# Second block of a two-block fp32 layer stack: the rescaled residual, the query parts and the sums of squares on VectorE, and five output tiles begun ahead of the attention norm

## The chip, the cores and the metric

The program runs on one core of a Trainium2 chip. The metric is device time in microseconds of the whole program. The time before is the median of three runs, and the profile is of a further execution. The engines are TensorE (PE: matmuls; PEld: its weight loads), VectorE (DVE), ScalarE (ACT), GpSimd (POOL) and SyncE (SP), which issues the DMAs. TensorE runs at one of two clocks, 2.4 or 1.2 GHz; the profile shows the granted one as a share of the full.

## The reference, cut to what matters

The input passes through two layers of a first block, which ends in a norm, then through one layer of a second block, on 512 tokens of width 1024, and at the end a mixture of experts. The second block, where the change is, computes:

```
h = rms_norm(x, ln1_w)                        # x: the first block's result, normed
xr, xg, q, k, v = split(h @ w_in)             # 512 columns each
y_rnn = gelu(xg) * scan(a, u)                 # u, a: gates of a convolved xr; h_t = a_t*h_(t-1) + u_t
y_att = softmax(q k^T / 8 + bias, causal by chunks of 64) v      # 8 heads of 64
x = x + concat(rms_norm(y_rnn, gn_rnn), rms_norm(y_att, gn_att)) @ w_out
x = x + cross_attention(rms_norm(x, ln2_w), rms_norm(mem))       # mem: 256 rows
out = norm(x + experts(rms_norm(x, ln3_w)))
```

## The kernel before, in words

Features lie on the 128 partitions and tokens along the row, so a tile is 128 x 512. A product of two fp32 matrices is made of parts: each operand is split into a rounded high part (ScalarE copies it) and a remainder (subtracted on another engine), and `mm3` adds three matmuls: high by high (line 183), and the two mixed ones (lines 184 and 185). The parts of weights come from `weights` (lines 165 to 180): SP loads a 128x512 piece, ScalarE makes the high part `wh` (line 176), POOL subtracts for the low part `wl` (line 177); the pool has four buffers of each. The parts of data come from `split` (lines 196 and 197) and `scaled_split` (203 and 204), on ScalarE and VectorE. `add_sq` squares a tile on ScalarE (209) and adds it to a sum on POOL (211), or on VectorE if it is told to. A norm is `tok_cols` (713: a matmul with ones adds over the partitions, 4 columns), `rsqrt_cols` (719 on VectorE, 721 on POOL), `bcast` (727: four transposes on TensorE, 729: a copy on VectorE); its result multiplies tiles afterwards.

The second block goes in this order. Four convolutions (line 890 evicts a tile, 893 and 895 are the taps). Then two chains taken in turn: `rnn_gelu` and the query and key tiles of the first four heads (`qk`, two heads a call) beside `rnn_gates` and `rnn_scan`. In `qk` line 872 evicts the query tile; its high part is copied on ScalarE (875) and its remainder made on POOL (876). Line 877 evicts the key tile; lines 879 to 882 make its parts, `kl` on VectorE (881) and its copy on ScalarE (882). `rnn_scan` multiplies (950), scans (951), multiplies by the gelu (952) and adds the square to a sum, which `rnn_norm` uses later. Then the residual is rescaled, eight tiles by a column on ScalarE (1051) and by the broadcast norm on POOL (1052). Then the eight heads, four pieces each: `scores` (978 and 979 on TensorE, 983 adds the bias and takes the maximum on VectorE, 984 is the exponential, 986 the division on VectorE), and `transpose_p` and `outputs` of the piece before. Between them `fill` runs steps of other work by a table: the remaining `qk`, the memory's keys and values (`mem_prep`, `mem_k`, `mem_v`, which takes two accumulators for each half of the columns), and `rnn_norm`. After the last head comes the output projection: eight tiles, each over eight pieces of its input `Y`, four from the recurrence and four from the attention. The first two tiles' recurrent halves go first, then the attention's sum of squares and norm, the scaling of the four attention pieces (1081) and their splits, then the rest; line 1074 adds a tile to the residual.

PSUM has four pools: `pm` of three accumulators for projections, `ps` of two for scores, `px` of two for transposes, `po` of one for head outputs. A scheduler puts each engine's instructions into a fixed order when the program is built, which keeps to dependences but not to the order of the code; at run time each engine goes through its row, and an instruction that waits holds up all behind it on its engine.

Of the kernel before, what the change touches and what calls it, by code (L numbers as in the profile page):

```python
# [15 lines left out]
OP = mybir.AluOpType  # L16
# [111 lines left out]
def body(ctx, tc, a, out, stop=None, dbg=None):  # L128
# [564 lines left out]
    with ExitStack() as c2:  # L693
# [170 lines left out]
        def qk(pr):  # L864
            qs = [slab(F32R, S) for _ in range(2)]
            qf = slab(n=S)
            kf = slab(n=S)
            kh = [slab(F32R, S) for _ in range(2)]
            kl = [slab(F32R, S) for _ in range(2)]
            lo, hi = slice(0, 64), slice(64, 128)  # L870

            yield from proj_g(win(1024 + 128 * pr), X, lambda p: V.scalar_tensor_tensor(qf, p, 0.125, R12, op0=OP.mult,
                                                                                       op1=OP.mult))
            for i, (own, oth) in enumerate(((lo, hi), (hi, lo))):
                ACT(qs[i][own], qf[own], AF.Copy)
                G.tensor_tensor(qs[i][oth], qf[own], qs[i][own].bitcast(F32), op=OP.subtract)
            yield from proj_g(win(1536 + 128 * pr), X, lambda p: V.tensor_tensor(kf, p, R12, op=OP.mult))
            for i, (own, oth) in enumerate(((lo, hi), (hi, lo))):
                ACT(kh[i][own], kf[own], AF.Copy)
                ACT(kh[i][oth], kf[own], AF.Copy)  # L880
                V.tensor_tensor(kl[i][own], kf[own], kh[i][own].bitcast(F32), op=OP.subtract)
                ACT(kl[i][oth], kl[i][own].bitcast(F32), AF.Copy)
            for i in range(2):
                QK[2 * pr + i] = (qs[i], kh[i], kl[i])
# [60 lines left out]
        def rnn_scan():  # L945
            ACT(m24, m24, AF.Sqrt, scale=0.25)
            yield
            for m in range(4):
# [2 lines left out]
                V.tensor_tensor_scan(m2, av, it, 0.0, op0=OP.mult, op1=OP.add)  # L951
                V.scalar_tensor_tensor(it, m2, 0.5, rn["g", m], op0=OP.mult, op1=OP.mult)
                yr.append(it)
                rn["acc"] = add_sq(rn.get("acc"), it, S)
                yield

        def rnn_norm():
# [76 lines left out]

        def mem_v():
            for g in range(2):
                ps = [pm.tile([128, 512], F32, name="pm") for _ in range(2)]
                yield from tokens(lambda k: wmv((g, k)), Xm, 2, ps)
                MV.append([scaled_split(ps[j], rm[:, j:j + 1], n=512) for j in range(2)])

# [5 lines left out]
        Rm = bcast(rm, 2)  # L1046
        run(both(main, side, (2, 1)))
        fillers.extend([qk(2), both(qk(3), mem_prep(), (1, 1)), mem_k(), both(mem_v(), rnn_norm(), (2, 1))])
        for k in range(KT):

            ACT(x2(k), x2(k), AF.Identity, scale=C("final_norm_w")[:, k:k + 1])
            G.tensor_tensor(x2(k), x2(k), R1, op=OP.mult)
        prev = None
        for h in range(8):
            if h + 2 < 8:
                load_bias(h + 2)
            while h not in QK:
                fill()
            for i in range(4):
                e = scores(h, i)  # L1060
                fill(int(STEPS_2[h][i]))
                if prev is not None:
                    transpose_p(*prev)
                    if prev[1] == 3:
                        outputs(prev[0])
                prev = (h, i, e)
        wo = Ahead([(m, wcol(a["w_out_2"][0], 128 * m)) for m in range(8)])
        fill(1000)
        wo(0)
        transpose_p(*prev)  # L1070
        outputs(7)


        outs = [proj_g(wo(m), Y, lambda p, m=m: V.tensor_tensor(x2(m), x2(m), p, op=OP.add)) for m in range(2)]
        for g in outs:
            for _ in range(2):
                next(g)
        ya = [yat[k] for k in range(4)]
        Ra = bcast(rsqrt_cols(tok_cols(sumsq(ya)), 512))
        for m in range(4):  # L1080
            V.scalar_tensor_tensor(ya[m], ya[m], C("gn_att_w_2")[:, m:m + 1], Ra, op0=OP.mult, op1=OP.mult)
            Y[4 + m] = split(ya[m], n=S)
        nrm = Norm(C("ln2_w_2"), S)
        for m in range(8):
            run(outs[m] if m < 2 else proj_g(wo(m), Y, lambda p: V.tensor_tensor(x2(m), x2(m), p, op=OP.add)))
            nrm(m)
        if stop == "b2a":
            nc.sync.dma_start(dbg.rearrange("(k p) t -> p k t", p=128), hT)
# [794 lines left out]
```

## Time and profile before

| | before |
|---|---|
| median of 3 runs | 1425.4 us (1424.39 to 1425.71) |
| profiled execution, its own time | 1425.72 us |
| its span, first to last instruction | 1423.9 us |
| mean granted clock of TensorE | 0.984 |
| TensorE busy | 1353.4 us |
| VectorE busy | 683.4 us, 48% |
| ScalarE busy | 555.1 us, 39% |
| POOL busy | 440.1 us, 31% |

The stretch of the change runs from about 540 us (the end of the first block's norm) to about 815 us. Rows of the timeline give start, duration and count of a run of equal instructions, the engine, line, operation and tiles, and in brackets how long the engine had been idle before and what released it. A matmul's duration overlaps the next one's, so its price is the distance from start to start.

### The profile page before, as it was taken

Reading aid. Unit: us, or ns where it says so; the run is one execution under the profiler, and the core shown is the slowest. Engines: PE = TensorE matmul, PEld = TensorE weight load, DVE = VectorE, ACT = ScalarE, POOL = GpSimd, SP = SyncE. Lnnn points to the kernel's source line nnn. Section 1 sums busy time; section 2 is a strip of 40 time slices with the busy share of each in tenths; the row PEclk is TensorE's granted clock in tenths of the full one; section 3 lists DMA queues with packets and bytes.
Section 4 is the critical chain, followed back from the end, with each engine's and each line's share of the span. In section 5 each row is a group of like instructions: output and inputs, shape, how many; then the busy total and the mean of one; then the engine's idle time right before and its main releaser. Section 6 shows DMA issues by size and latency. Waiting matters only on the chain.

```text
span 1423.9 us, 21255 instructions
## 1 busy us (share of the span) xinstructions
PE 1353.4 (95%) x8236; PEld 1018.1 (71%) x8236; DVE 683.4 (48%) x1305; ACT 555.1 (39%) x1048; POOL 440.1 (31%) x363
## 2 busy tenths in 40 slices
PE   6999999999999999989999999979999999999996
PEld 5998999999899997767876788863454354354343
DVE  5656775455677636777766244252213123132224
ACT  5355554334555562667755344421111110111113
POOL 3432223743222488464477432512000000000002
PEclk9999999999999999999999999989999999999998
DMA  6321112332211242313345122959999999999994
GB/s 202 96 75 40 49 52 84 97 97 66 56 42 58 69 125 81 90 52 120 103 127 175 38 63 91 347 200 382 423 403 423 422 422 423 422 420 422 422 418 154
DMA packets 159288, 279.32 MB, mean 196 GB/s; under 512 B 15568, under 2 KB 127440, under 8 KB 135120
## 3 DMA queue, kind: packets, MB, share of 16 engines
q1 hardware_dynamic: 159184, 277.92, 53.0%
q8 instruction: 66, 1.08, 0.3%
q14 instruction: 38, 0.31, 0.1%
HBM read 275.79 MB, written 2.10 MB: 195 GB/s over the span
## 4 chain that ended last, share of the span: by engine, by line
PE 59%; DVE 7%; DMA 3%; ACT 2%; issue 1%; POOL 1%; DVEq 0%; SPq 0%; POOLq 0%; ACTq 0%
PE pga L1530 7%; PE pgb L1530 7%; PE pm L184 5%; PE pm L185 5%; PE pm L183 5%; PE pgs L1621 4%; PE pgz L1580 3%; PE pgy L1580 3%; PE pgs L1352 3%; PE p L183 2%; PE p L184 2%; PE p L185 2%; DMA ring<-in_expert_gate_w_dram 1%; DMA ring<-in_expert_up_w_dram 1%; DVE slab L197 1%
## 5 line engine op out<-in xcount | busy, mean ns | idle before, releaser
L177 POOL TENSOR_TENSOR wl<-wraw,wh 128x512 fp32r<-128x512 f32 (+1 forms) x248 | 328.1, 1332 | 457.1 <-ACT wh L176 425.2
L176 ACT ACTIVATE wh<-wraw 128x512 fp32r<-128x512 f32 (+1 forms) x248 | 150.6, 616 | 212.6 <-PE pm L184 49.8
L183 PE MATMUL pp<-slab,wh 128*128 128x264 f32 (+1 forms) x536 | 154.8, 290 | 7.6 <-ACT wh L176 6.8
L184 PE MATMUL pp<-slab,wh 128*128 128x264 f32 (+1 forms) x536 | 155.7, 291 | 2.9 <-DVE slab L204 2.7
L185 PE MATMUL pp<-slab,wl 128*128 128x264 f32 (+1 forms) x536 | 154.8, 289 | 1.0 <-POOL wl L177 1.0
L1788 POOL TENSOR_TENSOR ring<-xtok,sel 128x512 f32<-128x512 f32 x4 | 5.0, 1282 | 406.2 <-DVE xtok L1623 406.2
L185 PE MATMUL pm<-slab,wl 128*128 128x512 f32 (+1 forms) x320 | 121.5, 381 | 5.6 <-POOL wl L177 5.5
L184 PE MATMUL pm<-slab,wh 128*128 128x512 f32 (+1 forms) x320 | 120.9, 378 | 2.2 <-DVE slab L197 2.2
L183 PE MATMUL pm<-slab,wh 128*128 128x512 f32 (+1 forms) x320 | 121.1, 380 | 0.0
L183 PE MATMUL p<-slab,wh 128*128 128x264 f32 (+1 forms) x400 | 115.7, 289 | 3.3 <-DVE rs L247 1.6
L1530 PE MATMUL pga<-ring,xT 128*64 128x512 f32 x504 | 116.1, 596 | 0.0
L1530 PE MATMUL pgb<-ring,xT 128*64 128x512 f32 x512 | 113.7, 592 | 0.3 <-DMA ring<-in_expert_up_w_dram 0.3
L185 PE MATMUL p<-slab,wl 128*128 128x264 f32 (+1 forms) x400 | 113.1, 283 | 0.0
L184 PE MATMUL p<-slab,wh 128*128 128x264 f32 (+1 forms) x400 | 112.8, 282 | 0.0
L183 PEld LDWEIGHTS pp<-slab,wh 128*128 128x128 f32 x536 | 103.6, 194 | 8.0 <-ACT wh L176 6.8
L184 PEld LDWEIGHTS pp<-slab,wh 128*128 128x128 f32 x536 | 103.4, 193 | 4.7 <-DVE slab L204 4.2
L185 PEld LDWEIGHTS pp<-slab,wl 128*128 128x128 f32 x536 | 103.8, 194 | 1.5 <-POOL wl L177 1.5
L1530 PEld LDWEIGHTS pgb<-ring,xT 128*64 128x64 f32 x512 | 37.0, 137 | 73.6 <-issue 71.4
L1590 DVE SCALAR_TENSOR_TENSOR yl<-pgy,wcol,yh 128x512 fp32r<-128x512 f32 x16 | 12.0, 751 | 158.2 <-ACT yh L1589 158.2
L1530 PEld LDWEIGHTS pga<-ring,xT 128*64 128x64 f32 x504 | 35.4, 137 | 66.1 <-issue 65.6
L183 PEld LDWEIGHTS p<-slab,wh 128*128 128x128 f32 x400 | 75.5, 189 | 5.1 <-issue 1.7
L184 PEld LDWEIGHTS p<-slab,wh 128*128 128x128 f32 x400 | 75.4, 189 | 0.0
(412 smaller groups left out, 3007.6 us busy)
## 6 DMA issues: line engine op xcount, KB each, us to landing
ring<-in_expert_gate_w_dram SPq DMA_DIRECT2D x63, 1024.0 KB, 17.7
ring<-in_expert_up_w_dram SPq DMA_DIRECT2D x62, 1024.0 KB, 16.2
ring<-in_expert_down_w_dram SPq DMA_DIRECT2D x56, 1024.0 KB, 17.0
wraw<-in_w_in_dram SPq DMA_DIRECT2D x108, 256.0 KB, 2.9
wraw<-in_w_out_dram SPq DMA_DIRECT2D x48, 256.0 KB, 2.9
wraw<-in_xk_w_dram SPq DMA_DIRECT2D x16, 256.0 KB, 2.9
wraw<-in_xv_w_dram SPq DMA_DIRECT2D x16, 256.0 KB, 2.6
wraw<-in_xq_w_dram SPq DMA_DIRECT2D x16, 256.0 KB, 2.9
```

Source lines behind the costliest of these rows:

```text
L176: ACT(h, raw, AF.Copy)
L177: G.tensor_tensor(lo, raw, h.bitcast(F32), op=OP.subtract)
L183: mm(ps, lh, rh, start=first, stop=False)
L184: mm(ps, lh, rl, start=False, stop=False)
L185: mm(ps, ll, rh, start=False, stop=last)
L197: V.tensor_tensor(lo, x, h.bitcast(F32), op=OP.subtract)
L1352: mm(p, h3[:, i, 128 * k:128 * k + 128], sl_[i], start=i == 0 and z == 0, stop=i == 3 and z == 1)
L1530: mm(p[64 * z:64 * z + 64], xt[:, k, CAP * (q + z):CAP * (q + z) + 64], W(src, 2 * pr + z, k), start=k == 0, stop=k == KT - 1)
L1580: mm(ps[c // 512][64 * z:64 * z + 64, c % 512:c % 512 + n], hT_[:, k, 64 * z:64 * z + 64], W("d", 2 * pr + z, k, c, n), start=k == 0, stop ...
L1590: V.scalar_tensor_tensor(yl, p, w[:rows, 0:1], yh.bitcast(F32), op0=OP.mult, op1=OP.subtract)
L1621: mm(p, t[:, 128 * i:128 * i + 128], y, start=q == 0, stop=q == len(ys) - 1)
L1788: G.tensor_tensor(y[i][:, :512], xtok[:, i, :512], fnw[:, :512], op=OP.mult)
```

## The change

It has five parts. (1) The rescale of a residual tile, a ScalarE and a POOL operation, becomes one VectorE operation (line 1054), written in the loop over the heads, one a head. (2) The query remainders, line 876, move from POOL to VectorE. (3) The recurrence's sums of squares move to VectorE; the attention's are added head pair by head pair inside the loop, on VectorE, where before all four stood behind it. (4) The second half of the memory values takes its accumulators from `ps` instead of `pm`. (5) The output projection's weights come in halves, and the recurrent halves of five tiles (three in `pm`, two in `ps`) stand ahead of the attention norm, then the second halves.

```diff
@@ qk @@
                 ACT(qs[i][own], qf[own], AF.Copy)
-                G.tensor_tensor(qs[i][oth], qf[own], qs[i][own].bitcast(F32), op=OP.subtract)
+                V.tensor_tensor(qs[i][oth], qf[own], qs[i][own].bitcast(F32), op=OP.subtract)
@@ rnn_scan @@
-                rn["acc"] = add_sq(rn.get("acc"), it, S)
+                rn["acc"] = add_sq(rn.get("acc"), it, S, eng=V)
@@ mem_v @@
-                ps = [pm.tile([128, 512], F32, name="pm") for _ in range(2)]
+                ps = [(ps_ if g else pm).tile([128, 512], F32, name="ps" if g else "pm") for _ in range(2)]
@@ the rescale, the heads @@
-        for k in range(KT):
-
-            ACT(x2(k), x2(k), AF.Identity, scale=C("final_norm_w")[:, k:k + 1])
-            G.tensor_tensor(x2(k), x2(k), R1, op=OP.mult)
-        prev = None
+        prev = acc = None
         for h in range(8):
...
+            V.scalar_tensor_tensor(x2(h), x2(h), C("final_norm_w")[:, h:h + 1], R1, op0=OP.mult, op1=OP.mult)
...
                         outputs(prev[0])
+                        if prev[0] % 2:
+                            acc = add_sq(acc, yat[prev[0] // 2], S, eng=V)
@@ the output projection @@
-        wo = Ahead([(m, wcol(a["w_out_2"][0], 128 * m)) for m in range(8)])
+        def whalf(m, hf):
+            return lambda: weights(4, [(0, a["w_out_2"][0][512 * hf:512 * hf + 512, 128 * m:128 * m + 128])])
+        NF = 5
+        wo = Ahead([((m, hf), whalf(m, hf)) for ms in (range(NF),) + tuple((m,) for m in range(NF, 8))
+                    for hf in range(2) for m in ms])
...
-        outs = [proj_g(wo(m), Y, lambda p, m=m: V.tensor_tensor(x2(m), x2(m), p, op=OP.add)) for m in range(2)]
-        for g in outs:
-            for _ in range(2):
-                next(g)
+        def out_half(m, hf, p):
+            w = wo((m, hf))
+            for k in range(4):
+                mm3(p, w[k][0], w[k][1], Y[4 * hf + k][0], Y[4 * hf + k][1], hf == 0 and k == 0, hf == 1 and k == 3)
+        po = []
+        for m in range(NF):
+            po.append((pm if m < 3 else ps_).tile([128, 512], F32, name="pm" if m < 3 else "ps"))
+            out_half(m, 0, po[m])
         ya = [yat[k] for k in range(4)]
-        Ra = bcast(rsqrt_cols(tok_cols(sumsq(ya)), 512))
+        Ra = bcast(rsqrt_cols(tok_cols(add_sq(acc, ya[3], S, eng=V)), 512))
...
         for m in range(8):
-            run(outs[m] if m < 2 else proj_g(wo(m), Y, lambda p: V.tensor_tensor(x2(m), x2(m), p, op=OP.add)))
+            if m >= NF:
+                po.append(pm.tile([128, 512], F32, name="pm"))
+                out_half(m, 0, po[m])
+            out_half(m, 1, po[m])
+            V.tensor_tensor(x2(m), x2(m), po[m], op=OP.add)
```

Three places show how the rows of the engines change. The first is POOL at the start of the convolutions, before against after; `hT` is the residual.

```order
 L889 MEMSET slab 128x4
-L1052 TENSOR_TENSOR hT<-hT,slab 128x512 x2
-L177 TENSOR_TENSOR wl<-wraw,wh 128x512
-L1052 TENSOR_TENSOR hT<-hT,slab 128x512 x6
+L177 TENSOR_TENSOR wl<-wraw,wh 128x512 x2
 L889 MEMSET slab 128x4
-L177 TENSOR_TENSOR wl<-wraw,wh 128x512 x3
+L177 TENSOR_TENSOR wl<-wraw,wh 128x512 x2
 L889 MEMSET slab 128x4
```

The eight rescales leave POOL's row, and the weight subtractions follow one another. On VectorE the scheduler sets all eight of line 1054 right behind line 729's copies, ahead of the first eviction of line 890.

The second place is VectorE ahead of the first scores. Before:

```order
L950 TENSOR_TENSOR slab<-slab,m_6821 128x512 x2
L877 TENSOR_TENSOR slab<-pm,slab 128x512
L951 SCALAR_TENSOR_TENSOR m_6821<-slab 128x512 x2
L952 SCALAR_TENSOR_TENSOR slab<-m_6821,slab 128x512 x2
L881 TENSOR_TENSOR slab<-slab 64x512 x2
L872 SCALAR_TENSOR_TENSOR slab<-pm,slab 128x512
L877 TENSOR_TENSOR slab<-pm,slab 128x512
L881 TENSOR_TENSOR slab<-slab 64x512 x2
L983 ISA slab,st_7357<-ps,slab 128x128
```

And after:

```order
L950 TENSOR_TENSOR slab<-slab,m_6821 128x512 x2
L876 TENSOR_TENSOR slab<-slab 64x512 x2
L211 TENSOR_TENSOR slab<-slab 128x512
L877 TENSOR_TENSOR slab<-pm,slab 128x512
L951 SCALAR_TENSOR_TENSOR m_6821<-slab 128x512 x2
L952 SCALAR_TENSOR_TENSOR slab<-m_6821,slab 128x512 x2
L211 TENSOR_TENSOR slab<-slab 128x512
L881 TENSOR_TENSOR slab<-slab 64x512 x2
L872 SCALAR_TENSOR_TENSOR slab<-pm,slab 128x512
L211 TENSOR_TENSOR slab<-slab 128x512
L877 TENSOR_TENSOR slab<-pm,slab 128x512
L876 TENSOR_TENSOR slab<-slab 64x512 x2
```

Four query remainders and three sums are new in the row, partly ahead of the second pair of scans and of line 881.

The third place is TensorE at the attention norm. Before:

```order
L184 MATMUL pm<-slab,wh 128x512
L185 MATMUL pm<-slab,wl 128x512
L713 MATMUL px<-tab,slab 128x1 x4
L183 MATMUL pm<-slab,wh 128x512
L184 MATMUL pm<-slab,wh 128x512
L727 MATMUL px<-tab,rstd_8840 128x128 x4
L185 MATMUL pm<-slab,wl 128x512
```

Behind these stand nine more matmuls of the same tile, and then the first of the attention half. After:

```order
L184 MATMUL ps<-slab,wh 128x512
L185 MATMUL ps<-slab,wl 128x512
L713 MATMUL px<-tab,slab 128x1 x4
L727 MATMUL px<-tab,rstd_8871 128x128 x4
L183 MATMUL pm<-slab,wh 128x512 x3
L183 MATMUL ps<-slab,wh 128x512
L184 MATMUL pm<-slab,wh 128x512
L185 MATMUL pm<-slab,wl 128x512
```

The matmuls that stood between and behind lines 713 and 727 now stand ahead of them, 60 in place of 24, and four tiles instead of three begin on the first attention piece.

## Rows read from the trace of the kernel before

**Rows 1.** The page: busy us, share of the span, instructions.

```profile
PE 1353.4 (95%) x8236; PEld 1018.1 (71%) x8236; DVE 683.4 (48%) x1305; ACT 555.1 (39%) x1048; POOL 440.1 (31%) x363
```

**Rows 2.** Slices: length, busy PE, PEld, DVE, ACT, POOL (count), clock, DMA share, GB/s.

```profile
620.00:640.00 20.00, 13.96 (x54) 10.45 (x53) 16.37 (x17) 13.77 (x24) 17.43 (x11) 0.89 0.14 39
640.00:660.00 20.00, 19.71 (x87) 15.64 (x87) 11.61 (x34) 15.06 (x35) 9.72 (x10) 0.86 0.44 134
660.00:680.00 20.00, 18.85 (x105) 14.95 (x103) 17.48 (x55) 15.43 (x43) 6.67 (x7) 1.00 0.34 105
```

**Rows 3.** TensorE's waits, 540 to 815: us in total, times, longest.

```profile
PE pm L185 <- POOL wl L177: 5.5, 2, 3.2
PE px L994 <- DVE slab L986: 3.1, 5, 0.9
PE pm L183 <- DVE slab L204: 2.2, 1, 2.2
```

**Rows 4.** Timeline of TensorE at the convolutions: start, us, instruction, idle before.

```profile
559.89 0.39 PE L184 MATMUL pm<-slab,wh 128*128 128x512 f32 x1
...
562.57 0.50 PE L185 MATMUL pm<-slab,wl 128*128 128x512 f32 x1 [2.29 <-POOL wl L177]
562.91 0.39 PE L183 MATMUL pm<-slab,wh 128*128 128x512 f32 x1
563.14 0.40 PE L184 MATMUL pm<-slab,wh 128*128 128x512 f32 x1
...
563.87 0.63 PE L184 MATMUL pm<-slab,wh 128*128 128x512 f32 x1
...
567.26 0.40 PE L183 MATMUL pm<-slab,wh 128*128 128x512 f32 x1
```

**Rows 5.** Timeline of POOL there and ahead of the scores.

```profile
552.20 9.07 POOL L1052 TENSOR_TENSOR hT<-hT,slab 128x512 f32<-128x512 f32 x6
...
620.18 3.84 POOL L876 TENSOR_TENSOR slab<-slab 64x512 fp32r<-64x512 f32 x2 [4.10 <-issue]
...
626.12 3.40 POOL L177 TENSOR_TENSOR wl<-wraw,wh 128x512 fp32r<-128x512 f32 x2
```

**Rows 6.** Timeline of VectorE at the convolutions.

```profile
551.55 0.69 DVE L890 TENSOR_TENSOR slab<-pm,slab 128x512 f32<-128x512 f32 x1 [3.20 <-PE pm L185]
```

**Rows 7.** Timeline of TensorE ahead of and at the first scores.

```profile
624.26 0.39 PE L184 MATMUL pm<-slab,wh 128*128 128x512 f32 x1
627.88 0.50 PE L185 MATMUL pm<-slab,wl 128*128 128x512 f32 x1 [3.23 <-POOL wl L177]
...
628.70 0.63 PE L185 MATMUL pm<-slab,wl 128*128 128x512 f32 x1
...
631.69 0.31 PE L978 MATMUL ps<-slab 128*128 128x128 f32 x1
...
639.72 0.69 PE L978 MATMUL ps<-slab 128*128 128x384 f32 x1 [2.72 <-DVE st L983]
```

**Rows 8.** Timeline of VectorE ahead of the first scores.

```profile
618.20 1.26 DVE L952 SCALAR_TENSOR_TENSOR slab<-m,slab 128x512 f32<-128x512 f32 x2
...
621.19 3.91 DVE L951 TENSOR_TENSOR_SCAN m<-slab 128x512 f32<-128x512 f32 x2
625.02 3.36 DVE L952 SCALAR_TENSOR_TENSOR slab<-m,slab 128x512 f32<-128x512 f32 x2
...
639.36 0.29 DVE L983 CUSTOM_DVE_ANT_0 slab<-ps,slab 128x128 f32<-128x128 f32 x1
```

**Rows 9.** Timeline of ScalarE ahead of the first score.

```profile
630.10 0.63 ACT L882 ACTIVATE slab<-slab 64x512 fp32r<-64x512 f32 x1 [0.90 <-DVE slab L881]
```

**Rows 10.** Timeline of TensorE at the attention norm.

```profile
757.56 1.02 PE L713 MATMUL px<-tab,slab 128*128 128x1 f32 x8
...
759.92 0.65 PE L727 MATMUL px<-tab,rstd 128*128 128x128 f32 x4 [0.76 <-POOL rstd L721]
...
762.81 0.97 PE L183 MATMUL pm<-slab,wh 128*128 128x512 f32 x3
```

More of the change, by code (lines that the diff above doesn't have):

```diff
@@ L1065, in body @@
                         outputs(prev[0])
+                        if prev[0] % 2:
+                            acc = add_sq(acc, yat[prev[0] // 2], S, eng=V)
                 prev = (h, i, e)
-        wo = Ahead([(m, wcol(a["w_out_2"][0], 128 * m)) for m in range(8)])
+        def whalf(m, hf):
[3 more added lines that the diff above has]
+                    for hf in range(2) for m in ms])
         fill(1000)
-        wo(0)
+        wo((0, 0))
         transpose_p(*prev)
         outputs(7)
-        outs = [proj_g(wo(m), Y, lambda p, m=m: V.tensor_tensor(x2(m), x2(m), p, op=OP.add)) for m in range(2)]
-        for g in outs:
-            for _ in range(2):
-                next(g)
+        def out_half(m, hf, p):
[6 more added lines that the diff above has]
+            out_half(m, 0, po[m])
         ya = [yat[k] for k in range(4)]
-        Ra = bcast(rsqrt_cols(tok_cols(sumsq(ya)), 512))
+        Ra = bcast(rsqrt_cols(tok_cols(add_sq(acc, ya[3], S, eng=V)), 512))
         for m in range(4):
```

## The prediction

> **What bounds the kernel now.** I read the page first: TensorE is busy for 95% of the span [rows 1], so a microsecond counts only where TensorE stands still or runs at its lower clock. Then the busy time in slices of 20 us over the stretch that the change touches [rows 2]: TensorE has 13.96 of 20 us at 620 to 640, with a granted clock of 0.89, and 0.86 in the next slice, while VectorE is at 17.48 of 20 at 660 to 680. So two limits follow each other: late inputs ahead of the first scores, and a busy VectorE under the heads. The list of TensorE's waits [rows 3] names who is late: the low weight parts of POOL (line 177) 5.5 us in two waits, line 204's split 2.2 us in one, and the softmax scaling of line 986 3.1 us in five. Last I read each of these places engine by engine [rows 4 to 10]. At full clock a 128x512 matmul follows the one before after 0.23 us (562.91 to 563.14, rows 4).
>
> No instruction of TensorE changes place after about 815 us, and the expert weights' loads there wait for TensorE and POOL in turn; so I let what is won before pass to the end whole.
>
> **The change part by part.** The sum is made against the profiled execution, 1425.7 us, which is 0.3 above the median of the runs. Positive means time won.
>
> *A, the rescale (lines 1051 and 1052 become line 1054).* TensorE stands for 2.29 us ahead of 562.57, for a low weight part of POOL [rows 4]. POOL was in six rescales until 552.20 + 9.07 = 561.27 [rows 5]; the matmul just before, 559.89, already used the high part of that tile, so its data had come long before. From 559.89 to 562.57 are 2.68 us in place of 0.23: 2.45 lost. Then from 563.87 on the matmuls are at the lower clock until 567.26: eight of them in 3.39 us instead of 8 x 0.23 = 1.84, so 1.55 more. Together 4.0. In the new order nothing but splits stands in POOL's row here, so all of it goes: **+4.0**. VectorE takes eight two-input operations. The nearest row is line 952, the same operation on the same shape, 1.26 us for two, 0.63 each, while POOL was idle (its 4.10 idle us end at 620.18), and 3.36 for two, 1.68 each, beside a busy POOL [rows 5, 8]. That is 5.0 to 13.4 us, at a place where VectorE idled for 3.20 us before line 890's eviction at 551.55 [rows 6]. The eviction behind them comes 2 to 10 us late. It frees one of three accumulators, and a conv tile is 24 matmuls, 5.5 us: TensorE has two more tiles, 11 us, before it needs that buffer. So I cost it at nothing; if the cover failed it would cost what lies over 11 us. Line 1051's eight ScalarE operations were beside TensorE's work, and their going wins nothing.
>
> *B and C, ahead of the scores (line 876 and the recurrent sums to VectorE).* At B TensorE stands 3.23 us ahead of 627.88 for a low weight part [rows 7]; POOL had two line 876 operations from 620.18 (3.84 us), a sum of line 211 behind them, and only from 626.12 the splits [rows 5]. From 624.26 to 627.88 are 3.62 us in place of 0.23, 3.4 lost; the seven matmuls from 628.70 to 631.69 took 2.99 instead of 1.61 us at the lower clock, 1.4 more: B is worth 4.8. At C it stands 2.72 us ahead of 639.72 for the third score's buffer, which line 983 on VectorE had to empty, and the slice from 640 has a granted clock of 0.86, which is 2.8 us of 20 [rows 2, 7]: C is worth some 5.6.
>
> The POOL wait of B goes. But the first score (line 979) needs the low key part, which comes after the second recurrent scan on the same VectorE, and VectorE now has more ahead of it. By the new order and the rows of before [rows 8, 9]: the first two of line 952 end at 619.4, line 950 takes to 620.6; then, new, two of line 876 and one of line 211 (3 x 0.63) to 622.5, line 877 to 623.1, two scans 3.91 to 627.0, two of line 952 at 0.63 instead of 1.68 (POOL has less beside them) to 628.3, a sum to 628.9, line 881 at some 0.8 (an estimate between those same two prices) to 629.7, and line 882's copy of 0.63 on ScalarE to 630.3. Since squares, key copies and splits pass between ScalarE and VectorE there, each waiting for the other, I put the first score at 631.0. Before, it ran at 631.69 [rows 7]. TensorE, without B, is there after nine more matmuls at 0.23, at about 626.8. So B's wait isn't won: it becomes a wait of 4.2 us for the keys, with a low clock behind it, and only 0.7 is won there. Behind it line 881's second pair and line 983 come some 1.6 us earlier by the same chain (637.8 against 639.4), and TensorE, later than before relative to them, stands shorter at C. Lowest is the chain alone, 1.6; highest is that with C's low-clock spell gone, 1.6 + 2.8 = 4.4. I take the middle: **+3.0**.
>
> *D, under the heads.* VectorE gains four of line 876 and two of line 211, 6 x 0.63 = 3.8 us, where it is at 17.48 of 20 [rows 2]. ScalarE gets three squares earlier than before. Fully on TensorE's path that is -3.8. On the other side, POOL's operations no longer lie beside VectorE's, and of the 3.1 us that TensorE waits for line 986 [rows 3] half may go, +1.5. The middle of the two ends is about **-1.0**.
>
> *E, the second half of the memory values in other accumulators (line 1034).* TensorE's single wait of 2.2 us for line 204 [rows 3] is for an accumulator that the first half's split still reads. With another pool's buffers it goes; bounds 0 (the weights are as late) and 2.2. No weight part is named in that wait, so I take **+2.0**.
>
> *F, the output projection around the attention norm.* Before, 12 matmuls of a third tile stood between the sum over partitions (line 713, 757.56) and the first matmul that needs the normed half (762.81) [rows 10]; only 0.76 us was idle. Now 60 matmuls stand ahead of line 713 and none between, so the chain line 719, 721, 727, 729, the scaling and the split lies bare: 762.81 - 757.56 = 5.25 us, less 0.9 for line 713 and 0.4 for line 727, is 3.9 idle against 0.76: 3.1 lost, of which one more ready matmul behind (0.23) gives a little back. The 36 matmuls drawn ahead win nothing, because line 713 ran without a wait before as well; nor do the sums moved out of the tail, for the same reason. Bounds: -2.5, if only the 11 matmuls' own time is missed, and -4.1, if a low clock follows the wait of 2.4 us ahead of 762.81 as it follows A's 2.29 (1.55 more, of -2.5). I take **-3.1**.
>
> Sum: 4.0 + 3.0 - 1.0 + 2.0 - 3.1 = 4.9, so 1420.8 for the profiled execution and **1420.5** for the median.
>
> **The rivals.** *The keys keep both waits.* VectorE's chain ends no earlier, because the squares and sums now stand in its order and the scan shares with POOL's splits: B and C win nothing, 1.9 in all, 1423.5. For it speaks that the first score is late by VectorE in either order; against it, line 952's 3.36 us beside POOL [rows 8].
>
> *Both waits and both low-clock spells go.* 4.8 + 5.6 instead of 3.0 makes 12.3, 1413.1. It needs the first score at 627, before the scan can end by my chain; that speaks against it.
>
> *The other side: VectorE paces the heads.* If each moved operation meets a split of POOL, it costs 1.68 as the later pair of line 952 does [rows 8], 6 x 1.68 = 10.1 us under the heads with no relief elsewhere, and B and C stay at their low end: 4.0 + 1.6 - 10.1 + 2.0 - 3.1 = -5.6, 1431.0. It decides from a D of -4.5 on (no gain), and is slower by more than 0.2% from -7.4 on. For it: 17.48 of 20. Against it: the six operations leave POOL, so as many meetings go as come. The Trainium skill ("GPSIMD Engine Reference", section "8. Key points") says that GpSimd shares its SBUF interfaces with VectorE and that the contention is with VectorE instructions that have two SBUF inputs, or use a two-port mode; the moved operations all have two, so by that page they go on meeting the splits, which is this rival, and the pair at 0.63 and 1.68 agrees with it.
>
> *The rescale isn't what makes A late.* Then A is 0 and the sum 0.9, 1424.5. Against it speaks that POOL comes free at 561.27 and its next split is what TensorE waits for.
>
> **How the numbers follow.** The forecast 0.54, the first rival 0.22, the second 0.11, the third 0.08, the last 0.05. The bounds of the forecast alone, all at once, are 4.0 + 4.4 + 1.5 + 2.2 - 2.5 = 9.6 and 4.0 + 1.6 - 3.8 + 0 - 4.1 = -2.3; taken not quite so far they make 1416 to 1425.5. The range of 1414.0 to 1425.5 leaves out the second and third rivals, 0.19. About 0.2%, 2.85 us, is what a measurement of this kernel can tell from no change, so faster means under 1422.5: the second rival and 0.52 of the forecast's and the first rival's 0.76, in all 0.63; the same 0.29; slower 0.08.
>
> **What would show it.** In the changed trace: no TensorE wait for line 177 near 560 and no slice below 0.95 in clock there (A); ahead of the first line 978 a wait of about 4 us for a slab of ScalarE or VectorE instead of POOL's (B), and the third score before 639 minus A's gain (C); VectorE over 17.5 of 20 from 660 to 700 without more TensorE waits (D); no wait for line 204 ahead of the second memory-value half (E); and a gap of some 1.5 and one of 2.4 us around the second line 727 (F). The forecast is wrong if the first score is ready at 627 or only after 632, or if waits for lines 986 or 197 under the heads grow by more than 4 us.

## The result: slower, and what the profile after shows

The changed kernel takes 1433.3 us, median of five runs (1431.87 to 1434.52), against 1425.4 before: the ratio is 1.0057, with a 95% interval of 1.0043 to 1.0072, so 7.9 us slower. The profiled execution took 1434.52, its span is 1432.7, the mean granted clock 0.984 as before. TensorE is busy for 1355.2 us, VectorE 686.7 (48%), ScalarE 549.6 (38%), POOL 411.1 (29%). The forecast was 1420.5, faster.

Of TensorE's waits in the changed stretch these bear on the argument, with the columns of [rows 3]:

```profile
PE px L727 <- POOL rstd L721: 5.4, 2, 4.0
PE ps L978 <- ACT slab L880: 3.7, 1, 3.7
PE px L994 <- DVE slab L986: 3.7, 5, 1.5
PE pm L183 <- ACT slab L196: 2.2, 1, 2.2
PE pm L183 <- ACT slab L203: 1.8, 2, 1.3
```

For POOL's weight parts TensorE waits 0.9 us, once, in place of 5.5 [rows 3], and line 204's wait is gone. In their place stand two norms (line 721, 5.4 us against 2.4 before), the key copies (line 880) and the scaled memory parts (line 203). The slices, with the columns of [rows 2]; the last line is the kernel before from 680 to 700:

```profile
560.00:580.00 20.00, 15.96 (x66) 12.76 (x66) 17.83 (x22) 4.72 (x8) 7.67 (x10) 0.91 0.31 93
620.00:640.00 20.00, 14.91 (x59) 11.42 (x57) 18.07 (x21) 12.86 (x22) 7.76 (x5) 0.91 0.19 54
640.00:660.00 20.00, 18.00 (x90) 13.77 (x90) 14.79 (x42) 17.27 (x40) 5.85 (x7) 1.00 0.44 131
660.00:680.00 20.00, 18.15 (x104) 14.59 (x103) 14.74 (x40) 13.02 (x33) 7.60 (x8) 1.00 0.29 93
680.00:700.00 20.00, 16.37 (x103) 14.15 (x102) 13.55 (x47) 14.38 (x37) 1.70 (x4) 0.94 0.21 67
760.00:780.00 20.00, 16.43 (x76) 13.44 (x75) 5.27 (x9) 5.70 (x10) 7.43 (x6) 0.90 0.50 152
...
680.00:700.00 20.00, 17.90 (x135) 16.65 (x134) 16.19 (x48) 16.59 (x41) 9.17 (x9) 1.00 0.27 80
```

From 660 to 700 TensorE is busy less than before, and its clock falls to 0.94 in the second of these slices. But VectorE is busy less too: 14.74 against 17.48 in [rows 2], and 13.55 against 16.19. So what paces that stretch isn't VectorE's load.

To see where the time went, I compare the starts of the same instructions in two traces. The traces begin up to 2.0 us apart, so each difference is taken less that trace's own shift at the first norm sum (529.13 before), which lies ahead of all that the change touches. Negative is earlier than before. The columns are the sum of the memory norm (line 713, 572.11), the first score (631.69), the seventh (655.50), the twelfth (665.39), the last (724.72) and the sum of the next norm behind the output projection (813.41); the right column is the ratio of the times and its interval. The dash: the row stands elsewhere in that kernel. A trace is one execution; the last column of starts and the measured ratios agree within some 2.0 us.

| kernel | 572 | 632 | 655 | 665 | 725 | 813 | ratio (95%) |
|---|---|---|---|---|---|---|---|
| changed kernel | -4.2 | -0.9 | -1.9 | +3.4 | +6.2 | +7.6 | 1.0057 (1.0043, 1.0072) |
| rescale_alone | -4.2 | -0.4 | -1.4 | -1.4 | -1.1 | -1.1 | 1.0000 (0.9989, 1.0012) |
| query_rnn_sums | 0.0 | -1.0 | -2.0 | -2.0 | -1.0 | -0.8 | 0.9998 (0.9988, 1.0008) |
| att_sums_loop | 0.0 | +0.1 | -0.1 | +5.3 | +6.4 | +6.2 | 1.0047 (1.0030, 1.0063) |
| out_proj_part | 0.0 | +0.2 | -0.1 | -0.1 | 0.0 | +1.9 | 1.0009 (0.9999, 1.0019) |
| att_sums_m24 | 0.0 | 0.0 | 0.0 | -0.1 | +1.1 | +2.8 | 1.0014 (1.0004, 1.0025) |
| att_sums_60_slabs | 0.0 | 0.0 | -0.1 | +5.2 | +6.3 | +6.3 | 1.0058 (1.0043, 1.0072) |
| before_58_slabs | -1.7 | +1.4 | -0.6 | -1.1 | -1.1 | +0.5 | 1.0004 (0.9994, 1.0014) |
| order_only | 0.0 | 0.0 | 0.0 | +5.2 | +4.7 | +6.0 | 1.0045 (1.0031, 1.0060) |
| after_m24 | -4.2 | -1.0 | -2.0 | -2.1 | -0.6 | +1.4 | 1.0009 (1.0000, 1.0019) |
| rescale_memnorm2 | - | +0.9 | +0.6 | +0.6 | +0.9 | +2.7 | 1.0005 (0.9993, 1.0018) |
| rescale_late | -4.2 | -5.5 | -5.3 | -5.4 | -5.3 | +0.9 | 1.0007 (0.9998, 1.0017) |
| rescale_mid | -4.2 | -5.5 | -5.3 | -5.4 | -5.3 | -1.9 | 0.9982 (0.9973, 0.9991) |
| rescale_two | -4.1 | -5.6 | -5.4 | -5.5 | -5.3 | -4.9 | 0.9967 (0.9955, 0.9979) |
| two_p4 | -4.2 | -5.6 | -5.4 | -5.4 | -5.3 | -6.3 | 0.9964 (0.9950, 0.9977) |
| best | -4.2 | -5.1 | -6.1 | -6.2 | -4.9 | +1.1 | 1.0009 (1.0000, 1.0018) |
| mid_p4 | -4.2 | -4.7 | -5.4 | -5.4 | -5.3 | +0.6 | 1.0012 (1.0002, 1.0021) |
| mid_p4_split | -4.2 | -5.6 | -5.4 | -5.5 | -5.4 | +0.9 | 1.0003 (0.9994, 1.0012) |
| mid_all | -4.2 | -5.1 | -6.1 | -6.2 | -5.0 | +1.1 | 1.0010 (1.0001, 1.0019) |

In the first line 4.2 us are won at 572, 3.3 of them are gone by the first score, and 8.1 are lost under the heads between 655 and 725.

### The profile page after: what moved, and what is told of

The parts are those of the page before. It is cut to its first block, busy times and chain, and to the rows that moved or that the text cites. A ratio compares the mean times of both kernels' runs of the same rounds, so it can differ in the third digit from the quotient of the medians.

```text
span 1432.7 us, 21217 instructions
## 1 busy us (share of the span) xinstructions
PE 1355.2 (95%) x8236; PEld 1020.4 (71%) x8236; DVE 686.7 (48%) x1324; ACT 549.6 (38%) x1040; POOL 411.1 (29%) x344
## 4 chain that ended last, share of the span: by engine, by line
PE 45%; DMA 3%; DVE 2%; ACT 2%; POOL 1%; issue 1%; DVEq 0%; SPq 0%; POOLq 0%; ACTq 0%
PE pga L1545 7%; PE pgb L1545 7%; PE pgs L1636 4%; PE pgz L1595 3%; PE pgy L1595 3%; PE pgs L1367 3%; PE pm L183 3%; PE pm L184 3%; PE pm L185 3%; DMA ring<-in_expert_up_w_dram 1%; DMA ring<-in_expert_gate_w_dram 1%; POOL wl L177 1%; PE po L183 1%; PE ps L183 1%; PE po L184 1%
## 5 line engine op out<-in xcount | busy, mean ns | idle before, releaser
L183 PE MATMUL pm<-slab,wh 128*128 128x512 f32 (+1 forms) x304 | 115.6, 384 | 4.0 <-ACT slab L196 2.2
L185 PE MATMUL pm<-slab,wl 128*128 128x512 f32 (+1 forms) x304 | 114.8, 379 | 0.0
L184 PE MATMUL pm<-slab,wh 128*128 128x512 f32 (+1 forms) x304 | 114.8, 379 | 0.0
```

What stands on the lines that cost most here:

```text
L183: mm(ps, lh, rh, start=first, stop=False)
L184: mm(ps, lh, rl, start=False, stop=False)
L185: mm(ps, ll, rh, start=False, stop=last)
```

## The experiments

### One part at a time

Each part of the change put into the kernel before by itself, the last two together.

**rescale_alone**, part 1 alone:

```diff
-        for k in range(KT):
-            ACT(x2(k), x2(k), AF.Identity, scale=C("final_norm_w")[:, k:k + 1])
-            G.tensor_tensor(x2(k), x2(k), R1, op=OP.mult)
...
+            V.scalar_tensor_tensor(x2(h), x2(h), C("final_norm_w")[:, h:h + 1], R1, op0=OP.mult, op1=OP.mult)
```

> The kernel before with the rescale alone as one VectorE operation a tile; TensorE's row is the same, word for word. My theory, from the two traces: the POOL wait of 2.3 us near 560 goes, but the memory norm's line 719, which stands in VectorE's row behind the convolutions, is no earlier, so TensorE waits 4 us instead of 1.1 for line 721 near 574 and falls to the lower clock there: nothing won, 1425.4 within 1. Rival, the forecast's step A: 4.0 won, 1421.4.

Measured: 1425.33 us, no difference. Its TensorE at the memory norm (columns of [rows 4]):

```profile
574.06 0.43 PE L727 MATMUL px<-tab,rstd 128*128 128x128 f32 x2 [4.04 <-POOL rstd L721]
```

The wait ahead of it was 1.14 us before and is 4.04 here, as in the changed kernel, whose VectorE and TensorE stand like this:

```profile
549.48 5.54 DVE L1054 SCALAR_TENSOR_TENSOR hT<-hT,cols,slab 128x512 f32<-128x512 f32 x5
554.94 0.68 DVE L890 TENSOR_TENSOR slab<-pm,slab 128x512 f32<-128x512 f32 x1
555.54 0.74 DVE L1054 SCALAR_TENSOR_TENSOR hT<-hT,cols,slab 128x512 f32<-128x512 f32 x1
...
573.28 0.68 DVE L890 TENSOR_TENSOR slab<-pm,slab 128x512 f32<-128x512 f32 x1
573.88 0.15 DVE L719 TENSOR_SCALAR ms<-px 128x2 f32<-128x2 f32 x1
```

```profile
570.42 0.40 PE L184 MATMUL pm<-slab,wh 128*128 128x512 f32 x1
574.86 0.69 PE L727 MATMUL px<-tab,rstd 128*128 128x128 f32 x2 [4.04 <-POOL rstd L721]
575.20 0.78 PE L185 MATMUL pm<-slab,wl 128*128 128x512 f32 x1
575.77 0.63 PE L183 MATMUL pm<-slab,wh 128*128 128x512 f32 x1
```

Line 719 stands in VectorE's row behind the fourth convolution's eviction. Before, it ran at nearly the same time, and TensorE came to the norm later:

```profile
573.21 0.15 DVE L719 TENSOR_SCALAR ms<-px 128x2 f32<-128x2 f32 x1
...
575.01 0.43 PE L727 MATMUL px<-tab,rstd 128*128 128x128 f32 x2 [1.14 <-POOL rstd L721]
```

So TensorE was 4 us earlier at the norm and waited there for what VectorE couldn't deliver earlier, with the lower clock behind it (0.63 a matmul). Five of the eight rescales stand ahead of line 890's first eviction and three among that tile's taps; it is not all eight that stand ahead, as the part on the change has it.

**query_rnn_sums**, parts 2 and the recurrent half of 3:

```diff
-                G.tensor_tensor(qs[i][oth], qf[own], qs[i][own].bitcast(F32), op=OP.subtract)
+                V.tensor_tensor(qs[i][oth], qf[own], qs[i][own].bitcast(F32), op=OP.subtract)
...
-                rn["acc"] = add_sq(rn.get("acc"), it, S)
+                rn["acc"] = add_sq(rn.get("acc"), it, S, eng=V)
```

> The kernel before with the query remainders and the recurrent sums alone on VectorE. If the forecast's steps B and C hold by themselves: 2 to 3 us won ahead of the scores and at most 1 lost under the heads, 1423 to 1424. Rival, VectorE paces the heads by load: the four query remainders there cost TensorE their 0.63 to 1.68 each, 2.5 to 6.7, so 1425.5 to 1430.

Measured: 1425.34, no difference that can be told, so the band of 1423 to 1424 is missed. By the table 2.0 us are won by the seventh score, and 1.2 given back by the end, 1.0 of them under the heads: the first theory's two figures for the stages, with an end that the times don't separate from nothing.

**att_sums_loop**, the attention's half of part 3:

```diff
                         outputs(prev[0])
+                        if prev[0] % 2:
+                            acc = add_sq(acc, yat[prev[0] // 2], S, eng=V)
...
-        Ra = bcast(rsqrt_cols(tok_cols(sumsq(ya)), 512))
+        Ra = bcast(rsqrt_cols(tok_cols(add_sq(acc, ya[3], S, eng=V)), 512))
```

> The kernel before with the attention's sums of squares alone moved into the loop over the heads. Theory one: ScalarE's square (line 209) stands in the row behind the head output that it needs, and holds up the softmax and the splits behind it; most of the 8 us that the changed kernel loses between the fourteenth piece and the recurrence's norm is this, 1429 to 1433. Theory two, load alone: two VectorE sums at 0.63 and three squares at 0.63, 1.3 to 3.2 us, 1426.7 to 1428.6. Theory three, they hide: 1425.4.

Measured: 1432.03, 6.7 slower: this part carries most of the 7.9. The size is that of theory one; whether the mechanism is, the runs of the next section tell.

**out_proj_part**, parts 4 and 5, as the diff of the change has them.

> The kernel before with the last two parts alone: the second half of the memory values in the other accumulators, and five recurrent halves ahead of the attention norm. Theory: the wait for line 204 (2.2 us) goes, the bare norm chain costs 3.1, so 1.1 lost, 1426.5. Rival, the half weights come late or the low clock follows the gap: 2 to 3 us more, 1428.5 to 1429.5.

Measured: 1426.46, 1.2 slower, with an interval that still includes 1, as the theory had it. In its trace the memory values' end is 1.4 us earlier (line 994 of the last head stands at 747.31 against 749.43, less a shift of 0.7) and 3.3 are lost behind that.

### What in the sums costs 6.7 us

**att_sums_m24**: the same squares and sums, in a buffer that the scan no longer needs:

```diff
+        def sq24(acc, pr):
+            sq = m24[:, pr]
+            ACT(sq, yat[pr], AF.Square)
+            if acc is not None:
+                V.tensor_tensor(sq, acc, sq, op=OP.add)
+            return sq
...
+                            acc = sq24(acc, prev[0] // 2)
...
-        Ra = bcast(rsqrt_cols(tok_cols(sumsq(ya)), 512))
+        Ra = bcast(rsqrt_cols(tok_cols(sq24(acc, 3)), 512))
```

> The attention's sums in the loop, as in the run that did this part alone (1432.0), with the same squares and sums, but written into a buffer that the scan has done with (m24) instead of into slabs. The order of TensorE's row then stays near that of before (65 lines of difference instead of 185). If the loss is the work itself or ScalarE's wait for the head output in its row: 1430 or more. If it is the pool of slabs, or the order that the scheduler makes of their release: 1425 to 1427.

Measured: 1428.36, a ratio of 1.0014 and so 2.0 us slower, a little outside the band of the second case, but far from the first. Its twelve runs lie between 1424.1 and 1429.4, so the 2.0 is loose, and what it is made of stays open. Theory one isn't borne out: in att_sums_loop as here each square under the heads starts at most 0.03 us behind the operation ahead of it. What waits for the head outputs is line 1013, which evicts them, and it did so before: from 640 to 735 ScalarE's idle time ahead of it is 9.2 us before, 9.0 here and 10.9 in att_sums_loop.

**att_sums_60_slabs** and **before_58_slabs**: `NSLAB = 59` becomes 60 with the sums in the loop, and 58 in the kernel before.

> The attention's sums in the loop in slabs, with 60 slabs instead of 59; the order of TensorE's row is the same, word for word, as with 59. If the missing slab is what instructions wait for at run time: back to 1425 to 1427. If it is the order: 1431 to 1433 as with 59.

> The kernel before with 58 slabs instead of 59; the order of TensorE's row is the same, word for word, as before. If the stages ahead of and under the heads live from the last slab: 1430 to 1433. If slabs are no limit: 1425.4 within 1.

Measured: 1433.20 with 60, 1426.23 with 58. One slab more doesn't mend it, one less doesn't cause it, so a missing slab at run time isn't what the 6.7 us are.

**order_only**: the work in the loop is left on one column, the real sums stay behind the loop:

```diff
+                        if prev[0] % 2:
+                            sqt = slab(n=S)
+                            ACT(sqt[:, :1], yat[prev[0] // 2][:, :1], AF.Square)
+                            if acc is not None:
+                                V.tensor_tensor(sqt[:, :1], acc[:, :1], sqt[:, :1], op=OP.add)
+                            acc = sqt
```

> The attention's sums in the loop again, with their slabs, but the squares and sums there on one column of 512 (their result isn't used; the real sums stand behind the loop as before). The work in the heads is gone, the order of TensorE's row stays far from that of before (179 lines of difference). If the order costs the 7 us: 1430 to 1433. If the work does: 1425 to 1427.

Measured: 1431.16, a ratio of 1.0045: with next to no work the loss is there. So it is the order that the scheduler makes, and not the work. The rows of VectorE and ScalarE change with TensorE's, and no run sets one of them alone; that the loss comes by TensorE's row is read from what follows. Counted in that row at full clock (0.23 us for 512 columns, 0.18, 0.12 and 0.06 for 384, 256 and 128), so much work (us) stands between the first score and the n-th:

| score | 11 | 12 | 13 | 16 | 20 | 21 | 22 | 23 | 27 | 32 |
|---|---|---|---|---|---|---|---|---|---|---|
| before | 22.9 | 23.8 | 25.0 | 33.4 | 38.0 | 41.1 | 43.2 | 45.3 | 58.2 | 73.4 |
| att_sums_m24 | 22.9 | 23.8 | 25.0 | 33.8 | 38.5 | 41.6 | 43.0 | 45.0 | 58.2 | 73.4 |
| att_sums_loop | 22.9 | 28.6 | 29.8 | 37.0 | 44.7 | 46.4 | 46.5 | 47.1 | 56.3 | 73.4 |
| order_only | 22.9 | 28.6 | 29.1 | 36.5 | 44.7 | 46.4 | 46.5 | 47.1 | 56.3 | 73.4 |

From the twelfth to the 23rd the scores stand up to 6.7 us later in the row, and the 20th to the 23rd nearly together (2.4 us of work from the first of them to the last, 7.3 before), with little work between them to hide their softmax. So the 5 us by which the twelfth score starts late are no loss yet: they are work that now stands ahead of it, 28.6 us against 23.8. At the last score the row holds 73.4 in all four, and there the +6.4 and +4.7 of the table are lost time; order_only loses another 1.3 behind the heads. The same in the slices from 655 to 727 (before, att_sums_loop, order_only, att_sums_m24) and from 690 to 700 (before, att_sums_loop):

```profile
655.00:727.00 72.00, 67.64 (x448) 59.63 (x447) 56.03 (x161) 54.26 (x136) 32.72 (x29) 1.00 0.35 108
655.00:727.00 72.00, 64.54 (x413) 55.83 (x412) 50.08 (x148) 52.02 (x127) 27.64 (x26) 0.98 0.32 100
655.00:727.00 72.00, 66.09 (x423) 57.31 (x422) 50.56 (x155) 52.59 (x132) 28.40 (x26) 0.98 0.32 99
655.00:727.00 72.00, 66.84 (x444) 58.59 (x443) 57.02 (x159) 55.29 (x137) 31.44 (x29) 1.00 0.34 104
```

```profile
690.00:700.00 10.00, 9.58 (x74) 9.25 (x75) 7.61 (x25) 7.86 (x22) 6.23 (x5) 1.00 0.28 81
690.00:700.00 10.00, 7.13 (x38) 5.91 (x37) 7.26 (x22) 8.67 (x22) 0.90 (x2) 0.83 0.19 55
```

With the scores close together TensorE is busy for 7.13 of 10 us and at a clock of 0.83. In the changed kernel it is the same place:

```profile
691.11 0.40 PE L978 MATMUL ps<-slab 128*128 128x512 f32 x1
691.34 0.40 PE L979 MATMUL ps<-slab 128*128 128x512 f32 x1
692.99 0.50 PE L183 MATMUL pm<-slab,wh 128*128 128x256 f32 x2 [1.25 <-ACT slab L203]
...
696.13 0.33 PE L978 MATMUL ps<-slab 128*128 128x128 f32 x1 [1.49 <-DVE st L983]
```

There TensorE stands 1.25 us for a scaled memory part and then 1.49 us for line 983, which has to empty a score's buffer.

**after_m24**: the changed kernel with the sums in m24, nothing else.

> The changed kernel, with the attention's squares and sums in m24 instead of slabs, all else as it is. If the scheduler's order under the heads is what makes the changed kernel slow, it goes from 1433.3 to about 1428 (the 1.2 of the output projection and up to 2 of the sums stay). If not: 1431 to 1434.

Measured: 1426.54, from 1433.3, a little better than expected: with the slabs, and the order that comes with them, go 6.8 us of the change's 7.9. Why the scheduler sets the scores so when the sums take slabs, at 59 or 60 alike, and not when they take m24, stays open; it settles that when the program is built, and no trace shows its reasons.

### Where step A's gain goes

**rescale_memnorm2**: rescale_alone, and the memory norm's reciprocal root issued ahead of the convolutions:

```diff
         R1 = bcast(r1)
+        rm = rsqrt_cols(tok_cols(macc, 2), D, 2)
...
-        rm = rsqrt_cols(tok_cols(macc, 2), D, 2)
         Rm = bcast(rm, 2)
```

> The rescale alone on VectorE, and the memory norm's reciprocal root (lines 713, 719, 721) issued ahead of the convolutions, where its sum has long been ready, so that line 727 needn't wait for line 719 behind the convolutions in VectorE's row. If that row's wait is what took the 4 us of step A: the wait and the low clock near 574 go, 4 won at 589, and 2 to 4 at the end: 1421.5 to 1423.5. Rival, the VectorE chain of the convolutions holds the gates anyway: 1425 within 1.

Measured: 1424.97, a ratio of 1.0005 (0.9993 to 1.0018), no difference. The wait moved on to the next thing behind the convolutions in VectorE's row:

```profile
577.49 0.80 PE L184 MATMUL pm<-slab 128*128 128x512 f32 x1 [4.14 <-DVE slab L197]
```

So it wasn't line 719 alone that was late, but what VectorE's row has behind the convolutions.

**rescale_late**: the eight operations held back behind the heads, in place of the old loop, by a column of scales that depends on the recurrence's last normed tile:

```diff
+        fw = sm.tile([128, 8], F32, name="fw", bufs=1)
+        V.scalar_tensor_tensor(fw, yr[3][:, 0:8], 0.0, C("final_norm_w"), op0=OP.mult, op1=OP.add)
+        for h in range(8):
+            V.scalar_tensor_tensor(x2(h), x2(h), fw[:, h:h + 1], R1, op0=OP.mult, op1=OP.mult)
```

> The rescale alone on VectorE, but held back by a column that depends on the recurrence's normed output, so that it runs behind the heads instead of ahead of the convolutions. If VectorE's row at the convolutions is what ate step A: no wait over 1.5 us and no low clock from 555 to 590, 4 us won there; behind the heads three of the eight operations stand ahead of line 204, and the wait there grows by 1 to 2: 1421 to 1424. Rival, something else in VectorE's convolutions paces: 1425 within 1.

Measured: 1425.45, a ratio of 1.0007: against the expectation no gain at the end. But the table has 5.3 won at 725. The convolutions are mended: the norm's wait is back at 1.14 us,

```profile
569.50 0.43 PE L727 MATMUL px<-tab,rstd 128*128 128x128 f32 x2 [1.14 <-POOL rstd L721]
```

and behind the heads the operations hold up what TensorE needs, first line 204's split (2.2 us in [rows 3]):

```profile
737.15 0.80 PE L183 MATMUL pm<-wh,slab 128*128 128x512 f32 x1 [3.51 <-DVE slab L204]
```

**rescale_mid**: the scales depend on the first half of the memory values' split instead, `MV[0][1][1]` in place of `yr[3]`; behind that split VectorE idled for 9.29 us before:

```profile
749.77 1.41 DVE L204 SCALAR_TENSOR_TENSOR slab<-pm,rstd,slab 128x512 fp32r<-128x512 f32 x2 [9.29 <-ACT slab L203]
```

> The rescale alone on VectorE, held back until the first half of the memory values is split, where VectorE idled for 9.3 us before; TensorE's row is the same, word for word, as before. If step A's gain is real and was given back only by the place that the operations took: 4 to 5.3 us, 1420 to 1421.5. If it is given back downstream anyway: 1425 within 1.

Measured: 1423.12, a ratio of 0.9982 (0.9973 to 0.9991): faster, by half of what was expected. VectorE there, and TensorE at the last head:

```profile
733.80 12.65 DVE L1068 SCALAR_TENSOR_TENSOR hT<-hT,fw,slab 128x512 f32<-128x512 f32 x8
746.38 1.39 DVE L204 SCALAR_TENSOR_TENSOR slab<-pm,rstd,slab 128x512 fp32r<-128x512 f32 x2
```

```profile
748.43 0.50 PE L184 MATMUL po<-ptl,slab 128*128 128x512 f32 x1 [1.45 <-DVE ptl L197]
```

Eight operations took 12.65 us, 1.58 each, beside POOL's weight splits: the upper price of the prediction (1.68), not the lower, so they overran the gap.

**rescale_two**: four tiles there, four behind the attention's last split (the second scales depend on `Y[7][1]`).

> The rescale on VectorE in two pieces: four tiles where VectorE idles behind the memory values' first half (4 x 1.6 = 6.4 us of 9.3), four behind the attention's splits, where their first reader is the fifth output tile. If the price of the place is all that ate step A, no wait for the last head's split is left: 4 to 5 us faster than before, 1420 to 1421.5. If the second piece holds up the first output tiles' additions: as in one piece, 1423.

Measured: 1419.92, a ratio of 0.9967 (0.9955 to 0.9979). Four operations fit, and VectorE idles again ahead of the next split:

```profile
733.83 5.85 DVE L1068 SCALAR_TENSOR_TENSOR hT<-hT,fw,slab 128x512 f32<-128x512 f32 x4
744.03 1.44 DVE L204 SCALAR_TENSOR_TENSOR slab<-pm,rstd,slab 128x512 fp32r<-128x512 f32 x2 [4.36 <-ACT slab L203]
```

**two_p4**: part 4 added to it.

> The same with the second half of the memory values in the other accumulators. If they add their 1.4: 1419 to 1420. If the scheduler's other order behind the heads costs more than that, as in one piece: 1421 to 1426.

Measured: 1419.65, a ratio of 0.9964 (0.9950 to 0.9977). In the table it is 1.4 ahead of rescale_two at 813, as expected; the times don't tell the two apart. It beats the kernel before by about 5.2 us, and the changed one by about 13.

### Combinations that gave nothing

**best**: rescale_late with parts 2, 4, 5 and the recurrent sums, and with one recurrent half set between lines 713 and 727 and one behind 727. **mid_p4**, **mid_p4_split**, **mid_all**: rescale_mid with part 4; with that same split of part 5 as well; and with the query and recurrent parts too.

```diff
-        for m in range(NF):
+        for m in range(3):
...
-        Ra = bcast(rsqrt_cols(tok_cols(sumsq(ya)), 512))
+        rs = rsqrt_cols(tok_cols(sumsq(ya)), 512)
+        for m in range(3, 4):
...
+            out_half(m, 0, po[m])
+        Ra = bcast(rs)
+        for m in range(4, NF):
...
+            out_half(m, 0, po[m])
```

> All that the runs speak for: the rescale held back behind the heads, query remainders and recurrent sums on VectorE, the memory values' other accumulators, five recurrent halves of which one stands between line 713 and line 727 and one behind it, and the attention's sums behind the loop as before. By the parts: 4 at the convolutions, 1 ahead of and under the heads, 1.4 at the memory values, 2 at the output projection: 1417 to 1420. Rival, VectorE's chain ahead of the first scores takes the 4 us back, since that chain ends no earlier: 1421 to 1423.

> The same, with the second half of the memory values in the other accumulators: 1.4 more by what the output projection's run showed in that stage, 1418.5 to 1420. If the order of the last heads, which the scheduler changes with it, costs as much: as without.

> The same with five recurrent halves as well, one of them between line 713 and line 727 and one behind line 727, three ahead: the bare norm chain's 3.3 goes and some of the waits for line 197 with it, 0 to 2 us more than mid_p4: 1417 to 1420.

> The same with the query remainders and recurrent sums on VectorE, so everything of the change but the attention's sums in the loop. By their own run they won 2 us at the first scores and lost 1 under the heads: 1416 to 1419. Rival, with the convolutions earlier the first scores wait longer for VectorE's chain and nothing is won: as mid_p4_split.

Measured: 1426.37, 1426.65, 1425.47 and 1427.43, with ratios of 1.0009, 1.0012, 1.0003 and 1.0010. All miss their bands. By the table they keep 4.9 us or more up to the last score and have lost all of it by 813. In all of them, as in rescale_mid, the eight rescales stand ahead of the last head's split in VectorE's row, and TensorE waits for that split: 5.6, 3.9, 4.3 and 4.2 us, where rescale_mid has 1.45 and rescale_two no such wait. No run takes that wait alone out of them. In mid_p4:

```profile
751.73 0.79 PE L184 MATMUL po<-ptl,slab 128*128 128x512 f32 x1 [3.89 <-DVE ptl L197]
```

## Why the prediction was wrong, step by step

**A, +4.0.** The size was right, 4.2 at 572. The step that failed is "so I cost it at nothing": it asked only whether line 890's eviction would hold up an accumulator (it didn't), and not what else stands behind the rescales in VectorE's row. That row paced the convolutions as soon as POOL didn't; TensorE waited 4.04 for line 721 instead of 1.14, and the lower clock followed (0.91 from 560 to 580, as before). At the first gate product behind it (line 184, 589.26 against 588.02, less the shift of 1.1) nothing of the 4.2 was left, and in rescale_alone A comes to nothing in time. The gain was real, as rescale_two shows, at another place for the eight operations. Of the signs for A, the wait for line 177 is gone as forecast, but the clock still falls below 0.95 there. The last rival (POOL isn't what is late) has A at 0 as it came out, but its mechanism is refuted by the 4.2.

**B and C, +3.0.** Of the right kind: the first score waits 3.74 for line 880, where 4.2 was forecast, and the third 1.45 instead of 2.72, and the clock from 640 to 660 is 1.00 instead of 0.86. In query_rnn_sums they win 2.0, inside the bounds of 1.6 to 4.4, and by the low clock that is gone rather than by an earlier third score (0.3 us later than before in the changed kernel, less the shift). VectorE's chain was priced right: the first score, forecast at 631.0, came at 631.93, which is 630.8 less the shift. But that chain was worked out from the rows of before, and A's 4.0 were added besides, as if VectorE came 4 us earlier with TensorE. It didn't, so at the first score nothing of A is left in the changed kernel. Even where the rescales stand elsewhere the two add up only in part: at the seventh score mid_all is 6.1 ahead and rescale_mid, which has no B and C, 5.3.

**D, -1.0.** The step that lost the prediction. 8.1 us went here, far beyond the lower bound of -3.8. It priced six VectorE operations, and took TensorE's row under the heads as it was. The four query remainders took back 1.0 us between 655 and 725 in query_rnn_sums, the step's own figure; the sums' work isn't the rest, since order_only loses nearly as much without it. The scheduler's order did it: after_m24 loses 1.4 in that stretch, so some 6.7 of the 8.1 went with the order. The work between the scores in the built rows was a term that the sum didn't have. The third rival had the side right and the mechanism wrong: VectorE's busy time fell to 14.74, so that its 1431.0 lies near the measured time is luck. The page that it leaned on, the Trainium skill's "GPSIMD Engine Reference", section "8. Key points", says that GpSimd shares its SBUF interfaces with VectorE and contends with VectorE operations of two SBUF inputs. The trace of rescale_mid agrees, 1.58 us each beside splits; it wasn't what cost the heads.

**E, +2.0, and F, -3.1.** In out_proj_part E gave 1.4, and F cost 3.3. E's wait for line 204 went; in its place TensorE stands 0.74 us for a low weight part, which the step's lower bound had named:

```profile
739.14 0.51 PE L184 MATMUL ps<-wl,slab 128*128 128x512 f32 x1 [0.74 <-POOL wl L177]
```

For F, the two gaps in the changed kernel are 1.34 and 2.23, forecast as 1.5 and 2.4:

```profile
774.86 0.65 PE L727 MATMUL px<-tab,rstd 128*128 128x128 f32 x4 [1.34 <-POOL rstd L721]
...
777.74 1.65 PE L183 MATMUL pm<-slab,wh 128*128 128x512 f32 x3 [2.23 <-ACT slab L196]
```

A slower stretch of clock stands behind (0.90 from 760 to 780, and 0.83 in out_proj_part), which the step had only in its lower bound. In out_proj_part seven matmuls take 2.99 us in place of 1.61:

```profile
771.35 0.63 PE L183 MATMUL ps<-slab,wh 128*128 128x512 f32 x1
...
774.34 0.47 PE L184 MATMUL pm<-slab,wh 128*128 128x512 f32 x1
```

But the waits for line 197 behind it fell from 2.2 us to 0.5, a term that the step didn't have either. So E's mechanism holds with a smaller size. F's bare chain holds as well; that its total came so close is in part luck, since two terms that it left out nearly cancel.

By parts alone: 0 for the rescale and for the queries, +6.7 for the sums in the loop and +1.2 behind the heads make 7.9, which is what the change costs.

## What to carry to other kernels

When a wait is taken from one engine by moving its work to another, look at what comes last in the receiving engine's row over the whole stage, not at the first buffer behind it: the place where the work stands decided between nothing and 5 us for the same eight operations. Where a scheduler sets the order, a line that costs next to nothing by itself can move everything behind it; compare the bottleneck engine's row over the whole stretch, by the work between landmarks, before pricing any instruction. And don't place a block of operations in an idle gap by their price alone in an idle machine.

## What the runs showed of the hardware

The same eight two-input VectorE operations on 128x512 tiles took 0.75 us each in rescale_late, where POOL stood idle until 739.59, and 1.74 to 1.78 in mid_p4, beside POOL's weight splits: more than twice as long. In rescale_mid the first, which began just ahead of POOL's first split, took 0.75, and the median of the eight was 1.78. In this order (least, median and greatest in ns):

```profile
L1068 DVE SCALAR_TENSOR_TENSOR hT<-hT,fw,slab x8: 745/748/753, 733.1 to 740.3; 128x512 f32<-128x512 f32 x8
L1068 DVE SCALAR_TENSOR_TENSOR hT<-hT,fw,slab x8: 1740/1774/1781, 736.1 to 748.0; 128x512 f32<-128x512 f32 x8
L1068 DVE SCALAR_TENSOR_TENSOR hT<-hT,fw,slab x8: 753/1777/1784, 733.8 to 744.7; 128x512 f32<-128x512 f32 x8
```

TensorE fell to its lower clock behind the 4.04 us wait ahead of 574.86, as it had behind one of 2.29 before; behind one of 2.18 ahead of 739.43, also before, it did not (1.00 from 740 to 760).
